# Memory keys of the last four sequences: transposed by VectorE inside one tile and scored on sixteen 32x32 tiles of the array, in place of TensorE transposes and column tiles; value products in two pieces

## The chip, the cores and the metric

The kernel runs on one core of a Trainium2 chip. The metric is device time in microseconds, the median of several runs. Engines are named as the profile names them: PE (TensorE matmul; PEld is its weight load), DVE (VectorE), ACT (ScalarE), POOL (GpSimd), SP (SyncE, which here mainly issues DMAs). Each has its own queue and takes its instructions strictly in the order of that queue.

## The reference, cut to what matters

The program is one layer of a decoder for a prompt group (1 sequence of 512 rows) and a sample group (8 sequences of 4 rows), with shared weights. The change touches the cross-attention alone, and there the sample group:

```python
def cross_attend(q, mk, mv):     # q (B, T, 4 heads, 256), mk and mv (B, 256 tokens, 4 heads, 256)
    s = einsum('bqhd,bmhd->bhqm', q, mk) * 256 ** -0.5
    return einsum('bhqm,bmhd->bqhd', softmax(s), mv)
```

For the prompt, `mk` and `mv` were computed earlier in the kernel. For each of the 8 sample sequences they lie in DRAM (`cache_mem_k`, `cache_mem_v`), 1 MB of keys and 1 MB of values each. A matmul contracts over the partitions, so the keys, which arrive with tokens on the partitions, must be turned so that the 256 dims of a head lie there.

## The kernel before, in words

The stage starts when the second half of the query projection ends and lasts until the output projection `w_mo`, whose first matmul in the trace is `mm<-wslot,oT`. Two streams of work are interleaved.

**The prompt** runs through a pipe of eight items (4 heads by 2 row blocks), one item a step at `next(prompt)`. `ch_soft` (L1357) makes 12 matmuls into `sca` (L1367), a row maximum on DVE (`cnm`, L1370), two exponentials on ACT (L1373), a reciprocal `csu` (L1374) and two multiplications `cp` on DVE (L1376). `ch_turn` (L1378) turns the result with 4 PE transposes `cpt` (L1385) and splits it into two parts with ACT and DVE (`pT`, L146 and L147). `ch_out` multiplies with the values (`cpo`, L1397) and evicts into `oT`.

**The samples**: `mk_load` (L1404) loads half a sequence's keys, 128 tokens x 1024, into a stage buffer `wst` (6 of them). `mk_turn` (L1409) turns that half with 8 PE transposes of 128x128 into `tpk` (L1416), copied into `kT` by ACT and DVE in turn (L1417). `kT` lives in the pool of weight slots, `W`, with four buffers. `mk_scores` (L1420) computes a sequence's scores with 8 matmuls on column tiles of the array, `128*32` in the profile (L1424). Then a maximum (`snm`, L1035) and an exponential (L1036). After the last sequence `sample_softmax` (L1039) turns and normalises the lot (`spa`, `spt`, `caz`). `mv_load` (L1428) loads values, for sequences 3 to 6 into slots of the same pool `W` (`vt`), else into stage buffers. `mv_out` (L1438) makes 8 matmuls a sequence into one accumulator `pso` (L1441). At the end ACT copies `pso` to `oS` (L1494) and PE turns it (`ost`, L1497) for the projection. 24 small loads (`cr`, L1509 to L1511) fetch convolution rows for the next sub-layer; they are issued by SP.

What sets the order: a tile scheduler places each instruction on its engine by a timeline of its own and by program order; `tc.issue_after` and `tc.high_priority` (the helper `burst`, L341) keep a group together behind a named instruction. PSUM banks come from two pools: `psm` with 5 banks (`sca`, `cpt`, `cpo`, `ssc`, `pso`) and `psa` with 3 (`tpk`, `spa`, `spt`, `ost`).

Of the kernel before, what the change touches and what calls it, by code (L numbers as in the profile page):

```python
# [18 lines left out]
NB = 8  # L19
# [58 lines left out]
def kernel(ctx: ExitStack, tc: tile.TileContext, I, O):  # L78
# [10 lines left out]

    cst = ctx.enter_context(tc.tile_pool(name="cst", bufs=1))  # L90
    sp = ctx.enter_context(tc.tile_pool(name="sp", bufs=11))
    wp = ctx.enter_context(tc.tile_pool(name="wp", bufs=NSLOT))
    stg = ctx.enter_context(tc.tile_pool(name="stg", bufs=6))
    npool = ctx.enter_context(tc.tile_pool(name="npool", bufs=5))
    t2p = ctx.enter_context(tc.tile_pool(name="t2p", bufs=8))
    zp = ctx.enter_context(tc.tile_pool(name="zp", bufs=3))
    sm = ctx.enter_context(tc.tile_pool(name="sm", bufs=4))
    psm = ctx.enter_context(tc.tile_pool(name="psm", bufs=5, space=bass.MemoryType.PSUM))
    psa = ctx.enter_context(tc.tile_pool(name="psa", bufs=3, space=bass.MemoryType.PSUM))
    dram = ctx.enter_context(tc.tile_pool(name="dram", bufs=1, space=bass.MemoryType.DRAM))  # L100
# [109 lines left out]
        return stg.tile([P, 1024], F32, name="wst", tag="st")  # L210

    def slot_tile():
        return wp.tile([P, 2, 1024], F32R, name="wslot", tag="W")

    def split_w(sv, st, share):

# [821 lines left out]
    def sample_softmax(sall, su, coef, sel, oname):  # L1038


        cf = small(NB, "scf")
        nc.vector.reciprocal(out=cf, in_=su)
        if coef is not None:
            VTS(out=cf, in0=cf, scalar1=coef, scalar2=None, op0=MUL)
        VTT(out=cf, in0=cf, in1=sel, op=MUL)
        VTT(out=view(csz, 0, [(64, NB // 2), (48, 2), (1, 16)]),
            in0=con("comb").unsqueeze(1).unsqueeze(1).broadcast_to([P, NB // 2, 2, 16]),
            in1=cf.rearrange("p (i e) -> p i e", e=2).unsqueeze(3).broadcast_to([P, NB // 2, 2, 16]), op=MUL)
        az = S([P, 2, H, NB * NS], F32, oname + "z")
        nc.gpsimd.memset(az, 0.0)  # L1050
        w = sall.shape[2]
        pa = at("spa")
        for e in range(2):
            for i in range(NB // 2):
                mm(pa[NS * i:NS * i + NS, :w], lhsT=csz[:, 2 * i + e, :], rhs=sall[:, 2 * i + e, :], start=(e == 0), stop=(e == 1))
        a = Z("spc")[:, :w]
        nc.scalar.copy(out=a, in_=pa[:, :w])
        pT = at("spt")
        for g in range(2):
            tr(pT[:, g * P:(g + 1) * P], a[:, g * P:(g + 1) * P], ident)  # L1060
        for g in range(2):
# [274 lines left out]
    qs = sm.tile([P, 8, NS], F32, name="qs", tag="qz", bufs=1)  # L1336
    qh, ql = [], []

    def ev_q(m):
        if m % 2 == 0:  # L1340
            qh.append(npool.tile([P, 2, 516], F32R, name="qh", tag="N"))
        if m % 4 == 0:
            ql.append(S([P, 4, SEQ], F32R, "ql"))

        def ev(i, c0, c1, ps):
            n = min(c1, SEQ) - c0
            q = qh[m // 2][:, m % 2, c0:c0 + n]
            nc.scalar.mul(out=q, in_=ps[:, :n], mul=1.0 / 16.0)
            STT(out=ql[m // 4][:, m % 4, c0:c0 + n], in0=ps[:, :n], scalar=1.0 / 16.0, in1=f32(q), op0=MUL, op1=SUB)
            if i == 1:  # L1350
                nc.scalar.mul(out=qs[:, m, :], in_=ps[:, n:n + NS], mul=1.0 / 16.0)
        return ev
# [3 lines left out]

    pTs, cps = {}, {}  # L1357

    def ch_soft(i):
        h, bp = i // 2, i % 2  # L1360
        sv = v2(mmp("sca"), 256)
        for j in range(2):
            t0 = (2 * bp + j) * P
            for c in range(2):
                q, l = qh[h][:, c, t0:t0 + P], ql[h // 2][:, 2 * (h % 2) + c, t0:t0 + P]
                for m, (x, k) in enumerate(((q, 0), (q, 1), (l, 0))):
                    mm(sv[:, j, :], lhsT=x, rhs=mkT[k][:, 2 * h + c, :], start=(c + m == 0), stop=(c == 1 and m == 2))  # L1367
        nm = small(2, "cnm")
        su = small(2, "csu")
        VRED(out=nm, in_=sv, axis=AX.X, op=MAX, negate=True)  # L1370
        p = cps[i] = v2(Z("cp"), 256)
        for j in range(2):
            ACT(out=p[:, j, :], in_=sv[:, j, :], func=AF.Exp, bias=nm[:, j:j + 1], accum_out=su[:, j:j + 1])  # L1373
        nc.vector.reciprocal(out=su, in_=su)  # L1374
        for j in range(2):
            VTS(out=p[:, j, :], in0=p[:, j, :], scalar1=su[:, j:j + 1], scalar2=None, op0=MUL)  # L1376
# [27 lines left out]
    def mk_load(i):  # L1404
        b, c = i // 2, i % 2
        kst[i] = stage()
        dma(out=kst[i], in_=I["cache_mem_k"][0, b, c * P:(c + 1) * P].rearrange("t h d -> t (h d)"))

    def mk_turn(i):  # L1409
        b, c = i // 2, i % 2  # L1410
        if c == 0:
            kts[b] = wp.tile([P, 8, 256], F32, name="kT", tag="W")
        for q in range(2):
            ps = at("tpk")
            for j in range(4):
                t = tr(ps[:, j * P:(j + 1) * P], kst[i][:, (4 * q + j) * P:(4 * q + j + 1) * P], ident)  # L1416
            (VCP if q else nc.scalar.copy)(out=kts[b][:, 4 * q:4 * q + 4, c * P:(c + 1) * P], in_=v2(ps, P))  # L1417
        return t.ins

    def mk_scores(b):  # L1420
        ps = mmp("ssc")[:, :256]
        for c in range(2):
            for h in range(H):
                t = mm(ps[NS * h:NS * h + NS], lhsT=qs[:, 2 * h + c], rhs=kts[b][:, 2 * h + c, :], start=(c == 0), stop=(c == 1))  # L1424
        sample_exp(sall, b, ps, nm, su)
        return t.ins

    def mv_load(b):  # L1428

        if 2 < b < 7:  # L1430
            t = wp.tile([P, 2, DM], F32, name="vt", tag="W")
            vts[b] = [t[:, 0], t[:, 1]]
        else:
            vts[b] = [stage(), stage()]
        for c in range(2):
            dma(out=vts[b][c], in_=I["cache_mem_v"][0, b, c * P:(c + 1) * P].rearrange("t h d -> t (h d)"))

    def mv_out(b):  # L1438
        for c in range(2):
            for h in range(H):  # L1440
                t = mm(pso[NS * h:NS * h + NS], lhsT=az[c][:, h, b * NS:(b + 1) * NS], rhs=vts[b][c][:, 256 * h:256 * h + 256],  # L1441
                       start=(b == 0 and c == 0), stop=(b == NB - 1 and c == 1))
# [51 lines left out]
    nc.scalar.copy(out=oS, in_=pso)  # L1494
# [10 lines left out]
    conv0 = I["state_conv"][0].rearrange("b j c -> (b j) c")

    def conv_in(t, p0, o, c0, n):

        dma(out=t[p0:p0 + 16, o:o + n], in_=conv0[:, c0:c0 + n])  # L1509
        dma(out=t[p0 + 16:p0 + 19, o:o + n], in_=I["w_dw"][0][:, c0:c0 + n])  # L1510
        dma(out=t[p0 + 19:p0 + 20, o:o + n], in_=I["b_dw"][:, c0:c0 + n])  # L1511


    cr = N("cr")
    for g in range(6):
        conv_in(cr, 20 * g, 0, 896 * g + (64 if g > 2 else 0), 896)
    conv_in(cr, 0, 896, 2688, 64)
    conv_in(cr, 0, 960, 5440, 64)
# [359 lines left out]
```

## Time and profile before

| quantity | value |
|---|---|
| time, median of 3 runs | 958.68 us (957.56 to 959.15) |
| time of the profiled execution | 957.37 us |
| its span in the trace | 955.6 us |
| from the first `sca` of this stage to the first `w_mo` matmul | 437.41 to 491.42 us |
| mean granted PE clock of the execution | 0.994 |

The span is what the profiler saw between the first and the last instruction; 1.8 us of the execution lie outside it. In a group line, the number behind `x` counts instructions, then come busy time and the mean duration of one in ns, then the idle time of the engine just before them with what ended it. In a timeline line, the first number is the start, the second the time until the last of the run of instructions ended. A matmul of fp32 is recorded as two passes, so 64 records are 32 matmuls. Records of matmuls overlap at their ends, so the cost of a run of them is read from its start to the next row's start.

### The profile page before, as it was taken

Reading aid. Unit: us, or ns where it says so; the run is one execution under the profiler, and the core shown is the slowest. Engines: PE = TensorE matmul, PEld = TensorE weight load, DVE = VectorE, ACT = ScalarE, POOL = GpSimd, SP = SyncE. Lnnn points to the kernel's source line nnn. Section 1 sums busy time; section 2 is a strip of 40 time slices with the busy share of each in tenths; the row PEclk is TensorE's granted clock in tenths of the full one; section 3 lists DMA queues with packets and bytes.
Section 4 is the critical chain, followed back from the end, with each engine's and each line's share of the span. In section 5 each row is a group of like instructions: output and inputs, shape, how many; then the busy total and the mean of one; then the engine's idle time right before and its main releaser. Section 6 shows DMA issues by size and latency. Waiting matters only on the chain. (4 is left out here: it accounts for less than half of the span.)

```text
span 955.6 us, 17087 instructions
## 1 busy us (share of the span) xinstructions
PE 933.3 (98%) x6619; PEld 810.2 (85%) x6619; DVE 600.3 (63%) x1129; ACT 387.7 (41%) x750; POOL 196.4 (21%) x383
## 2 busy tenths in 40 slices
PE   8999999999999999999999999999999999999995
PEld 5899787889766778998767799989988997999974
DVE  6745145565886448635654769727758676676767
ACT  5655134344676357635544523332212222222232
POOL 6610000115432216300000454001110110110114
PEclk9999999999999999999999999999999999999998
DMA  8950023344825539946954743063053313512023
GB/s 296 296 178 1 1 88 136 88 131 137 275 82 171 173 100 346 289 137 188 344 195 115 206 133 88 4 177 89 4 144 82 119 26 81 162 48 89 24 92 116
DMA packets 120674, 130.27 MB, mean 136 GB/s; under 512 B 8568, under 2 KB 86233, under 8 KB 120593
## 3 DMA queue, kind: packets, MB, share of 16 engines
q1 hardware_dynamic: 114408, 125.69, 42.3%
q10 hardware_dynamic: 6184, 3.48, 1.2%
q8 instruction: 52, 0.85, 0.4%
q14 instruction: 30, 0.24, 0.1%
HBM read 112.22 MB, written 16.93 MB: 135 GB/s over the span
## 5 line engine op out<-in xcount | busy, mean ns | idle before, releaser
L146 ACT CAST wslot<-wst 128x1024 fp32r<-128x1024 f32 x125 | 130.8, 1050 | 261.3 <-issue 73.5
L477 PE MATMUL mm<-fT,wslot 128*128 128x256 f32 x1872 | 235.9, 288 | 0.0
L477 PEld LDWEIGHTS mm<-fT,wslot 128*128 128x128 f32 x1872 | 234.4, 188 | 1.8 <-issue 0.8
L147 DVE TENSOR_TENSOR wslot<-wst,wslot 128x1024 fp32r<-128x1024 f32 x125 | 154.4, 1238 | 91.8 <-ACT wslot L146 91.4
L1689 PE MATMUL mm<-wslot,act 128*128 128x512 f32 (+1 forms) x180 | 70.2, 391 | 0.0
L1690 PE MATMUL mm<-wslot,act 128*128 128x512 f32 (+1 forms) x180 | 70.0, 392 | 0.0
L1688 PE MATMUL mm<-wslot,act 128*128 128x512 f32 (+1 forms) x180 | 69.3, 387 | 0.0
L1596 POOL COPY cvo<-u 128x2 f32<-128x2 f32 x43 | 11.0, 256 | 204.7 <-DVE u L1594 194.6
L407 PE MATMUL mm<-wslot,hT 128*128 128x512 f32 x128 | 51.6, 403 | 0.0
L477 PE MATMUL mm<-hT,wslot 128*128 128x256 f32 (+1 forms) x384 | 51.0, 289 | 0.0
L409 PE MATMUL mm<-wslot,hT 128*128 128x512 f32 x128 | 51.0, 400 | 0.0
L408 PE MATMUL mm<-wslot,hT 128*128 128x512 f32 x128 | 50.7, 396 | 0.0
L1591 DVE TENSOR_TENSOR u<-mm,rsb 128x256 f32<-128x256 f32 x43 | 18.2, 424 | 51.0 <-PE mm L477 50.0
L477 PEld LDWEIGHTS mm<-hT,wslot 128*128 128x128 f32 x384 | 49.2, 188 | 0.5 <-issue 0.2
L1688 PEld LDWEIGHTS mm<-wslot,act 128*128 128x128 f32 x180 | 34.3, 191 | 8.0 <-issue 0.4
L1690 PEld LDWEIGHTS mm<-wslot,act 128*128 128x128 f32 x180 | 33.8, 188 | 7.2 <-issue 0.4
L1689 PEld LDWEIGHTS mm<-wslot,act 128*128 128x128 f32 x180 | 33.8, 188 | 7.2
L1608 ACT ACTIVATE c<-c 128x560 f32<-128x560 f32 x21 | 14.1, 672 | 56.5 <-DVE c L1602 56.5
L1602 DVE SCALAR_TENSOR_TENSOR c<-u,cvT,c 128x560 f32<-128x560 f32 x43 | 34.3, 798 | 0.9
L1601 DVE SCALAR_TENSOR_TENSOR c<-u,cvT,c 128x560 f32<-128x560 f32 x43 | 34.1, 793 | 0.2
L1701 DVE TENSOR_TENSOR yp<-mm,yp 128x512 f32<-128x512 f32 (+1 forms) x41 | 27.2, 674 | 5.1 <-PE mm L1690 5.0
L409 PEld LDWEIGHTS mm<-wslot,hT 128*128 128x128 f32 x128 | 24.1, 188 | 5.1
(474 smaller groups left out, 1863.8 us busy)
## 6 DMA issues: line engine op xcount, KB each, us to landing
wst<-in_w_up_dram SPq DMA_DIRECT2D x42, 512.0 KB
wst<-in_w_in_dram SPq DMA_DIRECT2D x28, 512.0 KB
wst<-in_w_down_dram SPq DMA_DIRECT2D x20, 512.0 KB
wst<-in_cache_mem_k_dram SPq DMA_DIRECT2D x16, 512.0 KB
wst<-in_w_mk_dram SPq DMA_DIRECT2D x8, 512.0 KB
xb<-in_x_prompt_dram SPq DMA_DIRECT2D x8, 512.0 KB
wst<-in_cache_dk_dram SPq DMA_DIRECT2D x16, 256.0 KB
wst<-in_cache_dv_dram SPq DMA_DIRECT2D x16, 256.0 KB
```

Source lines behind the costliest of these rows:

```text
L146: nc.scalar.copy(out=hi, in_=src)
L147: (eng or nc.vector).tensor_tensor(out=lo, in0=src, in1=f32(hi), op=SUB)
L407: mm(ps[b], lhsT=xt.hi(k, c0, c0 + n), rhs=s[:, 0, kk, :], start=(k == 0), stop=False)
L408: mm(ps[b], lhsT=xt.hi(k, c0, c0 + n), rhs=s[:, 1, kk, :], start=False, stop=False)
L409: return mm(ps[b], lhsT=xt.lo(k, c0, c0 + n), rhs=s[:, 0, kk, :], start=False, stop=(k == nk - 1))
L477: mm(ps[i], lhsT=s[:, l, k, :], rhs=x(k, c0, c1), start=(k == 0 and j == 0), stop=(k == 7 and j == 2))
L1601: STT(out=c, in0=u[:, 1:EXT - 1], scalar=w[1], in1=c, op0=MUL, op1=ADD)
L1602: STT(out=c, in0=u[:, 0:EXT - 2], scalar=w[0], in1=c, op0=MUL, op1=ADD)
L1688: mm(ps, lhsT=t[:, 0, c0:c0 + P], rhs=s[:, 0, i % 2, cs], start=st, stop=False)
L1689: mm(ps, lhsT=t[:, 0, c0:c0 + P], rhs=s[:, 1, i % 2, cs], start=False, stop=False)
L1690: return mm(ps, lhsT=t[:, 1, c0:c0 + P], rhs=s[:, 0, i % 2, cs], start=False, stop=en)
L1701: VTT(out=y, in0=ps, in1=y, op=ADD)
```

## The change

Keys of sequences 0 to 3 go as before. Behind their scores the pool of weight slots is closed, and one tile `kq` (128 partitions x 8 half sequences x 1024) is opened in its place. Eight loads bring the keys of sequences 4 to 7 into it with tokens on the partitions; eight DVE instructions turn it in place in blocks of 32x32. The queries `qs` are stored to DRAM and read back four times into `qrep`, which has every block of 32 dims at every quarter of the partitions. 128 matmuls of 32 x 32 (`ssq`) then contract over 32 dims each, on sixteen tiles of the array: the row group is the tokens' quarter, the column group the head. Four accumulators in four banks of `psm` receive them, and four copies, one reduction over the four sequences and four exponentials follow. Only then is the pool of slots opened again, and the values of sequences 3 to 6 can be loaded into it. The value products are issued in two runs, sequences 2, 1, 0 and then 7, 6, 5, 4, 3. The 24 `cr` loads are issued by ACT's queue during the query projection.

```diff
-    wp = ctx.enter_context(tc.tile_pool(name="wp", bufs=NSLOT))
+    opened("w", NSLOT)
+    ctx.callback(lambda: closed("w"))
...
+    def conv_rows(g):
+        p0, o, c0, n = (20 * g, 0, 896 * g + (64 if g > 2 else 0), 896) if g < 6 else (0, 896 + 64 * (g - 6), 2688 + 2752 * (g - 6), 64)
+        for q0, m, src in ((0, 16, conv0), (16, 3, I["w_dw"][0]), (19, 1, I["b_dw"])):
+            nc.scalar.dma_start(out=cr[p0 + q0:p0 + q0 + m, o:o + n], in_=src[:, c0:c0 + n])
...
+    def kq_load(b):
+        for c in range(2):
+            dma(out=kq[:, b - 4, c], in_=I["cache_mem_k"][0, b, c * P:(c + 1) * P].rearrange("t h d -> t (h d)"))
+
+    def kq_turn(b):
+        for c in range(2):
+            nc.vector.transpose(kq[:, b - 4, c], kq[:, b - 4, c])
+
+    def kq_scores(t):
+        ps = [mmp("ssq") for _ in range(4)]
+        kt = kq.rearrange("p b c (j r) -> p (b c) j r", r=NS)
+        for j in range(8):
+            for i in range(4):
+                r = slice(NS * i, NS * i + NS)
+                for h in range(H):
+                    with burst(t):
+                        t = mm(ps[i][NS * h:NS * h + NS, :256], lhsT=qrep[r, 2 * h + j // 4, j % 4, :], rhs=kt[r, :, 8 * h + j, :],
+                               start=(j == 0), stop=(j == 7)).ins
+        for i in range(4):
+            (VCP if i % 2 else nc.scalar.copy)(out=sall[:, 4:8, :].rearrange("p b (c i r) -> p b c i r", c=2, i=4)[:, :, :, i, :],
+                                               in_=ps[i][:, :256].rearrange("p (b c r) -> p b c r", c=2, r=NS))
+        VRED(out=nm[:, 4:8], in_=sall[:, 4:8, :], axis=AX.X, op=MAX, negate=True)
+        for b in range(4, 8):
+            ACT(out=sall[:, b, :], in_=sall[:, b, :], func=AF.Exp, bias=nm[:, b:b + 1], accum_out=su[:, b:b + 1])
...
     next(prompt)
     for b in range(4):
-        t = mk_scores(b)
-    with tc.issue_after(t):
-        for j in range(8, 16):
-            t = mk_turn(j)
-            if j + 6 < 2 * NB:
-                mk_load(j + 6)
-            if j == 11:
-                next(prompt)
-    for b in range(3):
-        mv_load(b)
-    next(prompt)
-    with tc.issue_after(t):
-        for b in range(4, NB):
-            t = mk_scores(b)
+        with tc.issue_after(t):
+            mk_scores(b)
+    mv_load(0)
+    closed("w")
+    opened("k", 1)
+    kq = lay["k"][1].tile([P, 4, 2, DM], F32, name="kq", tag="K")
+    for b in range(4, NB):
+        kq_load(b)
+    dma(out=qs_d, in_=qs)
+    for i in range(4):
+        dma(out=qrep[NS * i:NS * i + NS], in_=qs_d.rearrange("(j q) m n -> q m j n", q=NS))
+    mv_load(1)
+    mv_load(2)
+    for b in range(4, NB):
+        kq_turn(b)
+    for _ in range(5):
+        next(prompt)
+    kq_scores(pe_last[0])
+    closed("k")
+    opened("w", NSLOT)
     for b in range(3, 7):
         mv_load(b)
     next(prompt)
-    _, az = sample_softmax(sall, su, None, con("selX"), "ca")
+    with tc.high_priority():
+        _, az = sample_softmax(sall, su, None, con("selX"), "ca")
...
-    for b in range(4):
-        mv_out(b)
-        if b == 0:
-            mv_load(7)
+    mv_out(VORD[:6])
+    mv_load(7)
     W.pump()
     next(prompt, None)
     next(prompt, None)
-    for b in range(4, NB):
-        mv_out(b)
+    mv_out(VORD[6:])
     run(prompt)
```

What the scheduler makes of it is seen in the order of the instructions; names are those of the program, output on the left, inputs on the right, and line numbers belong to each kernel's own source. On PE before, behind the scores of sequences 0 to 3, the transposes and scores of sequences 4 to 7 stand in this way:

```order
L1424 MATMUL ssc<-kT,qs 32x256 x27
L1416 MATMUL tpk<-cpk,wst 128x128 x12
...
L1367 MATMUL sca<-mkT,ql 128x256
L1416 MATMUL tpk<-cpk,wst 128x128 x40
L1424 MATMUL ssc<-kT,qs 32x256 x32
L1385 MATMUL cpt<-cpk,cp 128x128 x4
```

On PE after, at the same place, the prompt's items follow the scores at once, and the scores of sequences 4 to 7 come five `sca` groups later:

```order
L1438 MATMUL tpk<-cpk,wst 128x128 x4
L1476 MATMUL ssc<-kT,qs 32x256 x32
...
L1407 MATMUL cpt<-cpk,cp 128x128 x4
...
L1407 MATMUL cpt<-cpk,cp 128x128
...
L1389 MATMUL sca<-mkT,ql 128x256
L1463 MATMUL ssq<-kq,qrep 32x256 x128
L1419 MATMUL cpo<-pT,mvN 128x512 x12
```

So PE loses 64 transposes, and between the scores of the first four sequences (`ssc`) and those of the last four (`ssq`) it has prompt work alone: in all 60 `sca`, 16 `cpt` and 12 `cpo` matmuls.

On DVE after, from the maxima of the first four sequences on, the turns of `kq` stand among the prompt's small operations:

```order
L1392 TENSOR_REDUCE cnm<-sca 128x2
L157 TENSOR_TENSOR pT<-cpt,pT 128x256
L1453 STREAM_TRANSPOSE kq<-kq 128x1024
L1396 RECIPROCAL csu<-csu 128x2
L1392 TENSOR_REDUCE cnm<-sca 128x2
L157 TENSOR_TENSOR pT<-cpt,pT 128x256
L1398 TENSOR_SCALAR cp<-cp,csu 128x256 x2
L1453 STREAM_TRANSPOSE kq<-kq 128x1024 x2
...
L1453 STREAM_TRANSPOSE kq<-kq 128x1024
L1392 TENSOR_REDUCE cnm<-sca 128x2
L157 TENSOR_TENSOR pT<-cpt,pT 128x256
L157 TENSOR_TENSOR oT_5287<-cpo,oT_5286 128x512 x2
```

The first turn stands ahead of the `csu` and `cp` of the prompt's second item, and the second group of `cpt` on PE (the single row behind `...` above) reads that `cp`. Before, DVE had a copy of 512 columns (`kT<-tpk`) at such places.

On SP (the DMA issues) after, the order is this; before, the `cr` loads stood between the key loads, and `vt` followed the first six value loads directly:

```order
L1429 DMA wst<-in_cache_mem_k_dram 128x1024 x8
L1488 DMA wst<-in_cache_mem_v_dram 128x1024 x5
L1526 DMA qs_d<-qs 128x256
L1488 DMA wst<-in_cache_mem_v_dram 128x1024
L1528 DMA qrep<-qs_d 32x32x32 x4
L1449 DMA kq<-in_cache_mem_k_dram 128x1024 x8
L1129 DMA xb<-x_d_2549 32x1024
L1129 DMA xb<-x_d_2549 128x1024 x2
L1488 DMA vt<-in_cache_mem_v_dram 128x1024 x8
L1129 DMA xb<-x_d_2549 128x1024
L1488 DMA wst<-in_cache_mem_v_dram 128x1024 x2
```

The loads of `kq` now stand behind the store and the four reads of the queries, and `vt` behind `kq`.

More of the change, by code (lines that the diff above doesn't have):

```diff
@@ L97, with opened, closed @@
     sm = ctx.enter_context(tc.tile_pool(name="sm", bufs=4))
+    lay = {}
+    def opened(key, bufs):
+        c = tc.tile_pool(name=f"{key}{len(lay)}", bufs=bufs, side="right")
+        lay[key] = (c, c.__enter__())
+    def closed(key):
+        lay[key][0].__exit__(None, None, None)
+    opened("w", NSLOT)
+    ctx.callback(lambda: closed("w"))
     psm = ctx.enter_context(tc.tile_pool(name="psm", bufs=5, space=bass.MemoryType.PSUM))
@@ L212, in slot_tile @@
     def slot_tile():
-        return wp.tile([P, 2, 1024], F32R, name="wslot", tag="W")
+        return lay["w"][1].tile([P, 2, 1024], F32R, name="wslot", tag="W")
     def split_w(sv, st, share):
@@ L1185, in dk_turn @@
     def dk_turn(b):
-        kt = kts[b] = wp.tile([P, H, 260], F32, name="kT", tag="W")
+        kt = kts[b] = lay["w"][1].tile([P, H, 260], F32, name="kT", tag="W")
         nc.gpsimd.tensor_copy(out=kt[:, :, 256:260], in_=dkT[:, :, SEQ + TS * b:SEQ + TS * (b + 1)])
@@ L1337 @@
     qh, ql = [], []
+    conv0 = I["state_conv"][0].rearrange("b j c -> (b j) c")
+    cr = N("cr")
+    def conv_rows(g):
+        p0, o, c0, n = (20 * g, 0, 896 * g + (64 if g > 2 else 0), 896) if g < 6 else (0, 896 + 64 * (g - 6), 2688 + 2752 * (g - 6), 64)
+        for q0, m, src in ((0, 16, conv0), (16, 3, I["w_dw"][0]), (19, 1, I["b_dw"])):
+            nc.scalar.dma_start(out=cr[p0 + q0:p0 + q0 + m, o:o + n], in_=src[:, c0:c0 + n])
     def ev_q(m):
@@ L1357 @@
     pTs, cps = {}, {}
+    pe_last = [None]
     def ch_soft(i):
@@ L1366, in ch_soft @@
                 for m, (x, k) in enumerate(((q, 0), (q, 1), (l, 0))):
-                    mm(sv[:, j, :], lhsT=x, rhs=mkT[k][:, 2 * h + c, :], start=(c + m == 0), stop=(c == 1 and m == 2))
+                    pe_last[0] = mm(sv[:, j, :], lhsT=x, rhs=mkT[k][:, 2 * h + c, :], start=(c + m == 0), stop=(c == 1 and m == 2)).ins
         nm = small(2, "cnm")
@@ L1411, in mk_turn @@
         if c == 0:
-            kts[b] = wp.tile([P, 8, 256], F32, name="kT", tag="W")
+            kts[b] = lay["w"][1].tile([P, 8, 256], F32, name="kT", tag="W")
         for q in range(2):
@@ L1418, in mk_turn @@
         return t.ins
+    qrep = S([P, 8, 4, NS], F32, "qrep")
+    qs_d = dram.tile([P, 8, NS], F32, name="qs_d")
+    def kq_load(b):
[20 more added lines that the diff above has]
+            ACT(out=sall[:, b, :], in_=sall[:, b, :], func=AF.Exp, bias=nm[:, b:b + 1], accum_out=su[:, b:b + 1])
     def mk_scores(b):
@@ L1430, in mv_load @@
         if 2 < b < 7:
-            t = wp.tile([P, 2, DM], F32, name="vt", tag="W")
+            t = lay["w"][1].tile([P, 2, DM], F32, name="vt", tag="W")
             vts[b] = [t[:, 0], t[:, 1]]
@@ L1436, in mv_load, with mv_out @@
             dma(out=vts[b][c], in_=I["cache_mem_v"][0, b, c * P:(c + 1) * P].rearrange("t h d -> t (h d)"))
-    def mv_out(b):
-        for c in range(2):
+    VORD = [(b, 1 - c if b in (2, 7) else c) for b in (2, 1, 0, 7, 6, 5, 4, 3) for c in range(2)]
+    def mv_out(bs):
+        t = None
+        for b, c in bs:
             for h in range(H):
-                t = mm(pso[NS * h:NS * h + NS], lhsT=az[c][:, h, b * NS:(b + 1) * NS], rhs=vts[b][c][:, 256 * h:256 * h + 256],
-                       start=(b == 0 and c == 0), stop=(b == NB - 1 and c == 1))
-        return t.ins
+                with burst(t):
+                    t = mm(pso[NS * h:NS * h + NS], lhsT=az[c][:, h, b * NS:(b + 1) * NS],
+                           rhs=vts[b][c][:, 256 * h:256 * h + 256], start=((b, c) == VORD[0]), stop=((b, c) == VORD[-1])).ins
     sall = S([P, NB, 256], F32, "cas")
@@ L1453 @@
             for j in (i // 2 - 1, i // 2):
-                mk_turn(j)
-                mk_load(j + 6)
+                t = mk_turn(j)
+                if j < 2:
+                    mk_load(j + 6)
+            conv_rows(i // 2 - 1)
+            conv_rows(i // 2)
     next(prompt)
     for b in range(4):
-        t = mk_scores(b)
-    with tc.issue_after(t):
-        for j in range(8, 16):
-            t = mk_turn(j)
-            if j + 6 < 2 * NB:
-                mk_load(j + 6)
-            if j == 11:
-                next(prompt)
-    for b in range(3):
-        mv_load(b)
-    next(prompt)
-    with tc.issue_after(t):
-        for b in range(4, NB):
-            t = mk_scores(b)
+        with tc.issue_after(t):
[18 more added lines that the diff above has]
+    opened("w", NSLOT)
     for b in range(3, 7):
@@ L1504 @@
     cvT = S([P, NUT, 20], F32, "cvT")
[L1505 to L1518, printed above, removed]
     for t0 in (0, 4):
```

## The prediction, on record before the changed kernel was run

> **What bounds the kernel now.** I read the busy shares first, then PE's waits, then the timeline of this stage on PE, DVE and SP.
>
> ```profile
> PE 933.3 (98%) x6619; PEld 810.2 (85%) x6619; DVE 600.3 (63%) x1129; ACT 387.7 (41%) x750; POOL 196.4 (21%) x383
> PE ost L1497 <- ACT oS L1494: 1.5, 1, 1.5
> 458.30:472.50 14.20, 14.20 (x107) 12.12 (x103) 10.11 (x26) 8.97 (x35) 0.00 (x0) 1.00 1.02 409
> ```
>
> PE is busy 98% of the span. In the middle of this stage (third line, a window of 14.20 us: PE, PEld, DVE, ACT, POOL busy, granted clock, DMA share, GB/s) it is busy all the time, and DVE for 10.1 us. So a microsecond taken off PE here is a microsecond of time, as long as nothing else becomes late. The only wait of note in the stage is 1.5 us at its end, for the eviction of the samples' output (second line). The DMA engines are full in that window, at 409 GB/s: 512 KB take 1.28 us there.
>
> **What PE loses.**
>
> ```profile
> 439.00 1.05 PE L1424 MATMUL ssc<-kT,qs 128*32 128x256 f32 x10
> 439.99 0.65 PE L1416 MATMUL tpk<-cpk,wst 128*128 128x128 f32 x4
> 440.57 3.22 PE L1424 MATMUL ssc<-kT,qs 128*32 128x256 f32 x54
> 443.72 1.53 PE L1416 MATMUL tpk<-cpk,wst 128*128 128x128 f32 x12
> 445.01 0.48 PE L1367 MATMUL sca<-mkT,qh 128*128 128x256 f32 x2
> 446.50 0.60 PE L1385 MATMUL cpt<-cpk,cp 128*128 128x128 f32 x4
> 446.86 0.48 PE L1367 MATMUL sca<-mkT,qh 128*128 128x256 f32 x2
> 447.18 0.60 PE L1416 MATMUL tpk<-cpk,wst 128*128 128x128 f32 x4
> 447.53 0.37 PE L1367 MATMUL sca<-mkT,ql 128*128 128x256 f32 x1
> 447.74 1.03 PE L1416 MATMUL tpk<-cpk,wst 128*128 128x128 f32 x8
> 448.53 0.48 PE L1367 MATMUL sca<-mkT,qh 128*128 128x256 f32 x2
> 449.68 5.09 PE L1416 MATMUL tpk<-cpk,wst 128*128 128x128 f32 x40
> 454.70 3.66 PE L1424 MATMUL ssc<-kT,qs 128*32 128x256 f32 x64
> 458.29 0.66 PE L1385 MATMUL cpt<-cpk,cp 128*128 128x128 f32 x4
> ```
>
> From start to the next start, the 64 transposes (rows of 12, 4, 8 and 40) take 1.29 + 0.35 + 0.79 + 5.02 = **7.45 us**, all removed. The 64 records of the last four sequences' scores take 3.59 us; `ssq` takes their place. The first four sequences' scores stand in two pieces of 0.99 and 3.15 us, 4.14 in all; in one piece they should take 3.59 too, a gain of **0.55**.
>
> ```profile
> 472.55 0.62 PE L1441 MATMUL pso<-wst,caz 128*32 128x256 f32 x2
> 473.10 0.55 PE L1385 MATMUL cpt<-cpk,cp 128*128 128x128 f32 x3
> 473.57 2.58 PE L1441 MATMUL pso<-wst,caz 128*32 128x256 f32 x43
> 477.16 0.66 PE L1385 MATMUL cpt<-cpk,cp 128*128 128x128 f32 x4
> 485.93 0.85 PE L1441 MATMUL pso<-vt,caz 128*32 128x256 f32 x11
> ```
>
> A piece of value products with 2 records takes 0.55 us, one with 62 (three rows more, up to 477.16) 3.59: 0.051 a record, and 0.45 for going to column tiles and back. There are six pieces, the last at 485.93; two remain, which saves 4 x 0.45 = **1.8**. The wait of 1.5 for `oS` goes too: `ost` stands behind 18 matmuls of `w_mo`. Together 7.45 + 0.55 + 1.8 + 1.5 = **11.3 us** off PE.
>
> `ssq` has 128 matmuls in 8 rounds of 16 tiles. A round of four column tiles (eight records) took 3.59 / 8 = 0.45 us; if all sixteen run beside each other, eight rounds take 3.59, no loss; if row groups run one after another, 4 x 3.59 = 14.4, a loss of 10.8. Between lies the issue of instructions:
>
> ```profile
> L962 PE MATMUL mlsi<-wst,qzm x64: 272/273/276, 230.1 to 231.7; 128*32 128x128 f32 x64
> ```
>
> 64 records in 1.6 us are 25 ns each, the fastest pace of small matmuls here; 256 records by it are 6.4 us, a loss of 2.8. I take no loss, since no row shows a limit there, and keep 2.8 and 10.8 for the range. The Trainium skill ("TensorE: Matmul & The Clock Gate", Part 3: Packing small matmuls) gives 10.6 times for 4x4 tiles and 3.07 times for four row tiles, so sixteen tiles would be 3.45 times as fast as four and `ssq` would take 4.2, an estimate 0.6 above mine; no run here shows sixteen tiles.
>
> **What replaces it.** The keys of the last four sequences can be loaded only when `ssc` has read the slots. In the new order 4 transposes (0.58) and then 64 records (3.59) follow 439.00: `ssc` ends at 443.2.
>
> ```profile
> 437.46 0.20 ACT L1351 ACTIVATE qs<-mm 128x32 f32<-128x32 f32 x1
> 474.26 1.80 SPq L1436 DMA_DIRECT2D wst<-in_cache_mem_v_dram  x2
> 474.20:475.20 1.00, 1.00 (x26) 0.61 (x20) 0.48 (x2) 1.00 (x5) 0.00 (x0) 1.00 0.06 16
> 475.20:476.20 1.00, 1.00 (x26) 0.57 (x22) 0.95 (x3) 0.04 (x1) 0.00 (x0) 1.00 0.96 147
> 476.20:477.20 1.00, 1.00 (x19) 0.41 (x11) 0.00 (x0) 0.00 (x0) 0.00 (x0) 1.00 0.86 352
> q10 hardware_dynamic: 2690, 1.98, 30.6%
> ```
>
> Two loads issued at 474.26 find the queues nearly empty; 16 + 147 + 352 KB have moved by 477.2, so a 512 KB load lands **2.9 us** after its issue. Ahead of `kq` stand the four reads of `qrep`, 4096 pieces of 128 B, 256 for each DMA engine. The last row (a queue in the DMA view of 40 to 60 us: packets, MB, share of 16 engines) prices a packet of 736 B: 0.306 x 16 x 20 / 2690 = 36 ns. One of 4 KB takes 160 at 409 GB/s. The line through both gives 14 ns at 128 B, 3.6 us in all; ends are 1.3 (by bytes) and 9.3 (36 ns each). `qs` is complete at 437.7; its store lands about 2.5 later, the reads flow some 2.3 after their issue, so they end at 442.5 + 3.6 = 446.1, and the first half of `kq` lands 1.3 later, **447.4**. By the ends: 446.1 and 453.1.
>
> DVE's first turn stands ahead of the `csu` and `cp` of the second item, and DVE works in order, so everything behind it waits for that landing.
>
> ```profile
> L147 DVE TENSOR_TENSOR wslot<-wst,wslot 128x1024 fp32r<-128x1024 f32 x125 | 154.4, 1238 | 91.8 <-ACT wslot L146 91.4
> L318 DVE TENSOR_SCALAR hN<-xb,rs 128x1024 f32<-128x1024 f32 x4 | 3.0, 751 | 2.3 <-POOL rs L304 2.3
> L1370 DVE TENSOR_REDUCE cnm<-sca 128x2 f32<-128x512 f32 x8 | 5.5, 690 | 3.7 <-PE sca L1367 3.6
> L147 DVE TENSOR_TENSOR pT<-cpt,pT 128x256 fp32r<-128x256 f32 x15 | 6.2, 421 | 4.1 <-ACT pT L146 3.9
> L1376 DVE TENSOR_SCALAR cp<-cp,csu 128x256 f32<-128x256 f32 x16 | 5.1, 350 | 0.2
> L1374 DVE RECIPROCAL csu<-csu 128x2 f32<-128x2 f32 x8 | 1.3, 161 | 1.2 <-ACT cp L1373 0.9
> 442.47 0.61 DVE L1376 TENSOR_SCALAR cp<-cp,csu 128x256 f32<-128x256 f32 x2
> ```
>
> No row shows a turn. I take the row of the same shape, 1.24 us, since the turn reads and writes 1024 elements of 4 bytes; the lower end is 0.75, the one-source row; the upper, by the 690 ns for 512 elements, is 1.38. Two `cp` of 0.35 take 0.61 together, so 0.09 of each instruction lies in the next one. A turn then costs 1.15, eight 9.2. Between the first and the last stand 3 `csu`, 2 `cnm`, 3 `pT`, 6 `cp`: 0.48 + 1.38 + 1.26 + 2.10 - 14 x 0.09 = 4.0. DVE runs without a gap from 447.4 to 447.4 + 13.2 = **460.6**. Then `ssq` needs four of the five banks of `psm`, which come free with one `cnm`, three `pT`, two `oT` (by the 690 row) and a `csu`: 2.9 more, **463.5**.
>
> PE has work for less. From 443.2 on: 60 `sca` (12 take 446.50 - 445.01 = 1.49, so 7.45), 16 `cpt` (4 take 0.36, so 1.44), 12 `cpo` (2.94 from this row):
>
> ```profile
> 468.14 2.94 PE L1397 MATMUL cpo<-pT,mvN 128*128 128x512 f32 x12
> ```
>
> Together 11.8: it would reach `ssq` at 455.0. It **idles 8.5 us** before `ssq`; the first part, from 443.2 + 1.49 + 0.36 + 1.49 = 446.5 to the first `cp` at 449.8, is one gap of 3.3.
>
> Behind `ssq` the chain to `spa` (two copies a side, a maximum over 1024 columns, four exponentials, `csz`) is about 4.8 us long, beside 4.7 of `cpo`, `cpt` and `sca`. The last two value loads (sequence 7) wait for stage buffers of the first run of products, land 3.8 later (2.9 + half of 1.80), and their products stand 1.7 behind that run: a wait of 0.4 to 2.1, by when the buffers come free. With the casts of `w_mo` behind them I take **1.5**, from 0.5 to 3. The `vt` loads start after `ssq`, at 467, take 8 x 1.28 + 2.9 and land by 481, some 2 us before their products: hidden; later landing of `kq` moves both. The `cr` loads cost ACT 24 issues of about 0.3 in the query projection, where ACT stood idle 5.73 us before a pair of evictions:
>
> ```profile
> 436.25 0.66 ACT L1348 ACTIVATE qh<-mm 128x256 fp32r<-128x256 f32 x2 [5.73 <-PE mm L477]
> ```
>
> Nothing for that. **Sum:** -11.3 + 8.5 + 1.5 = -1.3. The profiled execution took 957.37 (span 955.6, and 1.8 around it), so 956.1 by it; the median stands 1.3 higher at 958.68, so 957.4 by that. I predict **957.5**. The PE work removed is nearly all given back as waiting for DVE.
>
> **Rivals.** *Faster, about 954*: turns at 0.75 take 8 x 0.49 = 3.9 off DVE's chain, and the idle before `ssq` falls to 4.6. For it: a one-source row has that pace. Against it: a turn is no plain stream, and `cnm` with one source runs at 1.35 ns an element. Same sign, smaller: `qrep` done early, -1.3.
>
> *Slower, up to 963*: the small pieces of `qrep` hold up `kq`. Each us that the first half lands behind 447.4 is a us of PE's idle; from 450.5 on the kernel is slower by over 0.2%, and 453.1 gives +5.7. For it: 128 B is far below any packet that I could price; against: the reads are issued some 2 us before `kq`.
>
> *The change doesn't do what it says*: the sixteen tiles don't run together, +2.8 to +10.8, 960.3 to 968.3. The rows show four column tiles together, but no row groups.
>
> *The clock falls.*
>
> ```profile
> 6.00:8.20 2.20, 0.49 (x5) 0.25 (x3) 1.77 (x4) 1.73 (x5) 1.03 (x3) 1.00 1.08 342
> 8.20:11.60 3.40, 2.93 (x11) 2.69 (x12) 2.17 (x4) 2.67 (x6) 3.26 (x3) 0.51 1.04 386
> ```
>
> After a stretch in which PE did little, its granted clock stood at 0.51 for 3.4 us. After the gap of 3.3 the same would add at most half of 3.4, 1.7, but PE waits for DVE there anyway, so I expect 0 to 0.5 of it: 957.5 to 959.2. The Trainium skill (the same page, "Why this matters for your kernels") asks for no idle gaps of PE above about 3 us, and so speaks against this change; the rows above agree with it.
>
> **How the numbers follow.** Forecast 0.42 (955 to 960), faster rival 0.24, `qrep` 0.19, tiles 0.10, clock 0.05. About 0.2%, 1.9 us, is what a measurement can tell. Faster by more is below 956.8: 0.13 of the forecast and 0.22 of its rival, 0.35. Slower is above 960.6: 0.02, 0.17, 0.10 and 0.01, 0.30. The rest, 0.35, is the same. The range goes from 951.5 (cheap turns and no wait behind `ssq`) to 966 (slow `qrep` and the issue pace of `ssq` together).
>
> **What would show it.** Steps hold if `tpk` shrinks by 64 matmuls, PE waits once for 3 to 4 us for `cp` behind the first turn, DVE is gapless over eight turns of 1.1 to 1.3 us, `ssq` starts near 463 and takes 3.6 to 4.2 us, `pso` has two pieces, and `ost` no wait. It is wrong if the first turn starts after 449, if `ssq` takes over 5, if a turn is far from 1.24, or if PE waits over 3 us behind `ssq`.

## The result, and the profile after

| kernel | median us (lowest to highest) | against before | 95% interval |
|---|---|---|---|
| before | 958.89 (957.56 to 961.23) | | |
| changed | 965.98 (964.67 to 967.18) | 1.0072 | 1.0054 to 1.0089 |

The change makes the kernel slower by 7.1 us (0.7%). 957.5 was forecast; 965.98 lies at the upper edge of the range (966.0), on the other side of no change. The profiled execution of the changed kernel took 964.67 us, with a span of 962.9. One execution of a later experiment, e3, took 3218.84 us and is left out of its median.

The traces of the two kernels give a second measure. At the first `w_mo` matmul the kernel before still has ten `cpo` matmuls open and the changed kernel none, so the stage is better read from the start of the first `sca` to the end of the last `w_mo` matmul:

```profile
545.05 0.40 PE L409 MATMUL mm<-wslot,oT 128*128 128x512 f32 x1
551.99 0.39 PE L419 MATMUL mm<-wslot,oT 128*128 128x512 f32 x1
```

That is 545.45 - 437.41 = 108.04 us before (first line) and 552.38 - 439.40 = 112.98 after: 4.9 us of the 7.3 between the two profiled executions. The rest lies ahead of the stage (2.0) and behind it (0.4).

Three of PE's waits in the stage of the changed kernel (line waited at, what it waited for, us in total, times, longest). None of them was there before, and the 1.5 us for `ost` are gone:

```profile
PE cpt L1407 <- DVE cp L1398: 5.6, 1, 5.6
...
PE pso L1498 <- DMA wst<-in_cache_mem_v_dram: 1.2, 1, 1.2
...
PE ssq L1463 <- issue: 0.7, 1, 0.7
```

The timeline of PE in the stage shows where they lie:

```profile
439.40 0.48 PE L1389 MATMUL sca<-mkT,qh 128*128 128x256 f32 x2
...
441.44 3.66 PE L1476 MATMUL ssc<-kT,qs 128*32 128x256 f32 x64
445.03 0.51 PE L1389 MATMUL sca<-mkT,qh 128*128 128x256 f32 x2
...
448.31 0.28 PE L1389 MATMUL sca<-mkT,ql 128*128 128x256 f32 x1
454.15 0.45 PE L1407 MATMUL cpt<-cpk,cp 128*128 128x128 f32 x1 [5.56 <-DVE cp L1398]
454.25 0.78 PE L1389 MATMUL sca<-mkT,qh 128*128 128x256 f32 x2
...
468.49 4.64 PE L1463 MATMUL ssq<-kq,qrep 32*32 32x256 f32 x213
473.82 1.31 PE L1463 MATMUL ssq<-kq,qrep 32*32 32x256 f32 x43 [0.69 <-issue]
475.06 3.04 PE L1419 MATMUL cpo<-pT,mvN 128*128 128x512 f32 x12
...
493.70 1.07 PE L1498 MATMUL pso<-wst,caz 128*32 128x256 f32 x16 [1.15 <-DMA wst<-in_cache_mem_v_dram]
```

The 64 transposes are gone and the first scores stand in one piece (445.03 - 441.44 = 3.59). Then PE stands still for 5.6 us, until `cp` of the second item is there. `ssq` runs from 468.49 to 475.06, 6.57 us where 3.59 were forecast, with a break of 0.69 in it. `pso` waits 1.15 for sequence 7.

The starts of the single `ssq` records in the trace show where the 6.57 us go. Of the 255 steps from one start to the next, 240 are at most 60 ns long, 13.4 on average, close to the 14.0 that the forecast implies (3.59 / 256). The other 15, of 67 to 1059 ns, take 3.0 us together. So the sixteen tiles do work beside each other, but the stream stops. The longest, 1.06 us between the starts of the 213th record and the next, is the row with `issue`: PE waited for nothing that the profile shows. A DMA queue shows what it probably was:

```profile
q8 instruction: 53, 0.87, 0.4%
```

The count of this queue (packets, MB, share of 16 engines) goes with PE's instructions: 52 packets of 16 KB in the kernel before, where PE and PEld have 13238 instructions, and 53 here, where they have 256 more. One packet moved from 471.38 to 472.32, while `ssq` ran, and the stream resumes 1.5 us after it, at 473.82. The other six profiles with a whole `ssq` show the same: the stream resumes 1.3 to 1.5 us after a packet of this queue has landed. In e4, where 24 more matmuls stand ahead, the stop comes 25 records earlier. So PE most likely waited for its own next instructions. What makes the 14 shorter stops is open.

Why `cp` is late is read from SP and DVE. SP's issues (start, us until the last of the group is issued):

```profile
439.67 0.37 SPq L1526 DMA_DIRECT2D qs_d<-qs  x1
441.54 0.33 SPq L1488 DMA_DIRECT2D wst<-in_cache_mem_v_dram  x1
443.52 3.25 SPq L1528 DMA_DIRECT2D qrep<-qs_d  x4
446.94 4.13 SPq L1449 DMA_DIRECT2D kq<-in_cache_mem_k_dram  x8
```

and DVE's timeline, with the first and the last of the eight turns:

```profile
451.53 1.25 DVE L1453 STREAM_TRANSPOSE kq<-kq 128x1024 f32<-128x1024 f32 x1 [3.42 <-DMA kq<-in_cache_mem_k_dram]
452.70 0.12 DVE L1396 RECIPROCAL csu<-csu 128x2 f32<-128x2 f32 x1
452.75 0.67 DVE L1392 TENSOR_REDUCE cnm<-sca 128x2 f32<-128x512 f32 x1
453.33 0.41 DVE L157 TENSOR_TENSOR pT<-cpt,pT 128x256 fp32r<-128x256 f32 x1
453.66 0.60 DVE L1398 TENSOR_SCALAR cp<-cp,csu 128x256 f32<-128x256 f32 x2
...
457.20 0.69 DVE L1392 TENSOR_REDUCE cnm<-sca 128x2 f32<-128x512 f32 x1 [0.60 <-PE sca L1389]
...
464.08 1.24 DVE L1453 STREAM_TRANSPOSE kq<-kq 128x1024 f32<-128x1024 f32 x1
```

The four reads of the queries take SP 3.25 us to issue, 0.81 each, where `kq`'s eight take 4.13. Ahead of them SP stood still for 1.6 us, until the store `qs_d` had landed. So the first key load is issued at 446.94, 1.9 us after `ssc` ended, and lands 4.6 later, at 451.5. From there DVE works without a gap, but for 0.60, until 465.3; three operations of the prompt stand behind the first turn ahead of the `cp` that PE waits for. A turn takes 1.24 us, as forecast.

The windows of the gap and of what follows it (length, then PE, PEld, DVE, ACT and POOL busy, granted clock, DMA share, GB/s):

```profile
448.60:454.15 5.55, 0.00 (x0) 0.03 (x1) 2.62 (x6) 0.89 (x4) 0.00 (x0) 0.90 1.02 357
454.15:463.20 9.05, 8.59 (x32) 7.06 (x33) 8.45 (x14) 1.99 (x8) 0.00 (x0) 0.50 0.89 319
```

Behind the gap PE's granted clock is halved for 9 us (two `sca` take 0.78 instead of 0.48). DVE is busy for 8.45 of these 9.05 us, so little of it should reach the end; e4 tests that.

### The profile page after: what moved, and what is told of

Read it like the earlier page. It is cut to its first block, busy times and chain, and to the rows that moved or that the text cites. A ratio compares the mean times of both kernels' runs of the same rounds, so it can differ in the third digit from the quotient of the medians.

```text
span 962.9 us, 17322 instructions
## 1 busy us (share of the span) xinstructions
PE 932.9 (97%) x6747; PEld 808.6 (84%) x6747; DVE 602.9 (63%) x1128; ACT 384.2 (40%) x744; POOL 198.0 (21%) x383
## 4 chain that ended last, share of the span: by engine, by line
PE 80%; DVE 7%; DMA 6%; ACT 3%; issue 2%; POOL 1%; SPq 1%; DVEq 0%; ACTq 0%; POOLq 0%
PE mm L487 32%; PE mm L475 7%; PE mm L417 6%; PE mm L418 6%; PE mm L419 6%; PE mm L1739 3%; PE mm L1737 3%; PE mm L1738 3%; DMA wst<-in_w_mk_dram 2%; PE mm L396 1%; DVE wslot L157 1%; PE sda L1221 1%; DMA kq<-in_cache_mem_k_dram 1%; PE sdn L396 1%; PE oda L1247 1%
## 5 line engine op out<-in xcount | busy, mean ns | idle before, releaser
L314 POOL TENSOR_TENSOR rs<-ssy,mhalf 128x1 f32<-128x1 f32 (+1 forms) x10 | 6.4, 639 | 107.6 <-DVE ssy L1139 104.7
```

## The experiments

Times are medians, against the kernel before in the same series (958.9 to 959.3). "To ssq" is the time from the first `sca` of the stage to the first `ssq` in that kernel's profile, "ssq" from there to the next matmul, "stage" the time from the first `sca` to the end of the last `w_mo` matmul. The stage is one execution's; the two kernels that differ in the convolution loads alone, before and e8, agree in it to 0.04 us, while the times of single executions of one kernel spread over 2 to 8.

| kernel | us | against before, 95% interval | to ssq | ssq | stage |
|---|---|---|---|---|---|
| before | 958.89 | | | | 108.04 |
| changed | 965.98 | 1.0072 (1.0054 to 1.0089) | 29.1 | 6.6 | 112.98 |
| e2, keys issued first | 962.75 | 1.0033 (1.0021 to 1.0046) | 26.5 | 6.9 | 112.73 |
| e3, turns late | 963.57 | 1.0044 (1.0027 to 1.0061) | 27.3 | 7.8 | 112.55 |
| e4, gap filled | 964.41 | 1.0055 (1.0038 to 1.0072) | 28.7 | 6.8 | 112.10 |
| e5, ssq on half the columns | 970.40 | 1.0102 (1.0075 to 1.0128) | 29.5 | 7.1 | 119.23 |
| e9, half of the ssq matmuls | 961.67 | 1.0028 (1.0012 to 1.0043) | 29.4 | 3.3 | 109.37 |
| e11, keys and loads alone | 964.70 | 1.0062 (1.0039 to 1.0084) | 28.9 | 7.2 | 112.90 |
| e7, three mends | 960.56 | 1.0016 (1.0001 to 1.0031) | 25.7 | 6.4 | 108.61 |
| e1, value products alone | 957.91 | 0.9986 (0.9976 to 0.9995) | | | 105.72 |
| e6, e1 with sequence 7 last | 959.20 | 0.9998 (0.9984 to 1.0012) | | | 106.01 |
| e10, e1 with sequence 7 third | 957.62 | 0.9985 (0.9971 to 1.0000) | | | 105.39 |
| e8, convolution loads alone | 958.57 | 0.9993 (0.9976 to 1.0009) | | | 108.08 |

**The late landing: e2.**

```diff
     for i in range(4):
-        dma(out=qrep[NS * i:NS * i + NS], in_=qs_d.rearrange("(j q) m n -> q m j n", q=NS))
+        with tc.issue_after(kq_last[0]):
+            dma(out=qrep[NS * i:NS * i + NS], in_=qs_d.rearrange("(j q) m n -> q m j n", q=NS))
```

> The changed kernel with the four reads of the queries issued behind the eight key loads instead of ahead of them. Theory (late first landing): the first key load is issued when the scores of sequences 0 to 3 end (445.0 on the scale of the changed kernel's trace) and lands 2.9 us later, near 448 instead of 451.5; DVE is gapless from there, so the time falls by about 3.5 us to 962.5, and PE's wait for cp shrinks from 5.6 to about 2. Rival (DVE or the DMA rate bounds the turns whenever the first one lands, or the queries then come too late): 965 to 967.

SP and DVE in this kernel's timeline:

```profile
444.16 3.79 SPq L1449 DMA_DIRECT2D kq<-in_cache_mem_k_dram  x8
448.06 11.59 SPq L1531 DMA_DIRECT2D qrep<-qs_d  x4
```

```profile
447.85 1.25 DVE L1455 STREAM_TRANSPOSE kq<-kq 128x1024 f32<-128x1024 f32 x1 [0.86 <-DMA kq<-in_cache_mem_k_dram]
```

The first load is issued 0.2 us after `ssc` ends (at 443.9 there) and lands 3.7 later, where it was 1.9 and 4.6. PE's wait for `cp` falls to 3.0, and `ssq` starts 2.6 earlier. So the theory holds on the landing: the reads issued ahead of the keys made it late. What it gave at the end is less clear. The median falls by 3.2 us, close to the 3.5 expected, but in the trace the stage is only 0.25 shorter, because PE then waits 3.2 us for the values of sequence 7 instead of 1.15:

```profile
PE pso L1500 <- DMA wst<-in_cache_mem_v_dram: 3.2, 1, 3.2
```

Why the medians differ by more than this is not settled.

**The place of the turns: e3.**

```diff
-    for b in range(4, NB):
-        kq_turn(b)
     for _ in range(5):
         next(prompt)
+    for b in range(4, NB):
+        with tc.issue_after(cp_last[1]):
+            kq_turn(b)
```

> The changed kernel with the eight turns on DVE allowed only behind the cp of the prompt's second item. Theory (the length of DVE's chain from the first landing to the last turn decides): only some 1.2 to 1.6 us of small operations move ahead of the landing, so 964 to 965, though PE's single wait of 5.6 us breaks up. Rival (the blocked queue itself is the loss): the 5.6 us come back, near 960.5.

The single wait is gone, but new ones stand in its place on PE:

```profile
PE cpo L1421 <- DVE pT L157: 2.9, 1, 2.9
PE sca L1389 <- DVE kq L1455: 2.6, 1, 2.6
...
PE cpt L1409 <- DVE cp L1398: 1.5, 2, 1.1
```

2.4 us of the median come back, not 5.6, and `ssq` starts 1.8 earlier: the length of DVE's chain counts, and only what can be moved ahead of the landing shortens it. `ssq` itself, which starts at half clock and stops twice, takes 1.2 of the 1.8 back, and in the trace the stage is only 0.4 shorter.

**The halved clock: e4.** After the third `sca` group PE got 24 matmuls that nothing reads.

```diff
+        if k == 1:
+            gps = at("gap")
+            g = pe_last[0]
+            for _ in range(24):
+                with burst(g):
+                    g = mm(gps, lhsT=warm[:, 0:P], rhs=warm, start=True, stop=True).ins
```

> The changed kernel with 24 matmuls of 128x512 bf16 on zeros, without use, put on PE into the wait for the second item's cp, so that PE does not stand idle there. Theory (PE waits for DVE in this stretch whatever its clock): the granted clock stays at 1.0 behind the gap instead of 0.50 for 9 us, and the time falls by 1 us at most, 965 to 966. Rival (the halved clock is what the change loses): the 4.5 us of PE work lost at half clock come back, 961 to 962.

The row of e4 behind the gap (length, PE busy, granted clock, DMA share, GB/s):

```profile
458.00:462.00 4.00, 3.09 (x12) 0.72 0.78 221
```

The granted clock was 1.00 from 446 to 458 and 0.72 in the next 4 us, behind a wait of 1.6. The time fell by 1.6 us, which is more than the theory's 1 and far from the rival's 4.5; its interval overlaps with that of the changed kernel, and the scheduler moved a few prompt matmuls too. In the trace `ssq` starts 0.4 us earlier and the stage is 0.9 shorter, of which 0.8 is a shorter wait for sequence 7 (0.33). So by this run the clock costs at most 1.6 us, and by its trace less than 1.

**What ssq costs: e5 and e9.**

```diff
-                        t = mm(ps[i][NS * h:NS * h + NS, :256], lhsT=qrep[r, 2 * h + j // 4, j % 4, :], rhs=kt[r, :, 8 * h + j, :],
+                        t = mm(ps[i][NS * h:NS * h + NS, :128], lhsT=qrep[r, 2 * h + j // 4, j % 4, :], rhs=kt[r, 0:4, 8 * h + j, :],
```

> The changed kernel with each of the 128 ssq matmuls on 128 columns instead of 256: it leaves out the scores of sequences 6 and 7 and uses those of 4 and 5 in their place, so that only the time of ssq changes. Theory (the pace of issue bounds ssq: 256 records at about 22 to 25 ns each, whatever their columns): ssq stays near 6 us, from 5.5, and the time at 965 to 966. Rival (the columns are streamed, row groups partly one after another): ssq falls to about 3.3, and the time by some 3 us to 963.

PE in e5:

```profile
469.82 3.80 PE L1463 MATMUL ssq<-kq,qrep 32*32 32x128 f32 x213
475.65 1.35 PE L1463 MATMUL ssq<-kq,qrep 32*32 32x128 f32 x43 [2.03 <-issue]
```

213 records take 3.80 us, 17.8 ns each, against 4.64 and 21.8 on 256 columns. These two can't be compared as they stand, for the granted clock (the third number from the end) was not the same; the first line is from e5, the second from the changed kernel:

```profile
469.80:475.70 5.90, 3.87 (x222) 3.40 (x225) 1.48 (x4) 1.02 (x4) 0.00 (x0) 0.79 0.27 92
468.49:475.06 6.57, 5.88 (x257) 3.81 (x256) 2.31 (x7) 1.48 (x6) 0.00 (x0) 1.00 0.27 85
```

In e5 it stood at 0.50 for the first 2.2 us of `ssq`. The records 113 to 208 ran at full clock in both kernels; by their starts they follow each other at 13.1 ns in e5 and at 20.2 in the changed kernel. Half the columns save a third there, so the columns count too, and neither the theory nor the rival is right about the pace. All of `ssq` takes 7.1 us even so: the stop behind the 213th record grew from 1.06 to 2.30 us, and the first part ran at half clock. The packet of instructions starts to move 3.1 us into `ssq`, as late as in the changed kernel (2.9), but PE is then at its 184th record instead of its 145th, so that it runs out sooner. The time rose by 4.4 us, which neither foresaw. The granted clock behind `ssq` is 0.50, where it is 1.00 in the changed kernel:

```profile
477.00:481.00 4.00, 4.00 (x10) 3.14 (x11) 1.72 (x3) 2.35 (x10) 0.00 (x0) 0.50 0.69 206
```

That the longer stop lost the clock here is likely, since PE stood still for 2.03 us just ahead of it, but no run separates it from the rest.

```diff
-        for j in range(8):
+        for j in range(4):
...
-                               start=(j == 0), stop=(j == 7)).ins
+                               start=(j == 0), stop=(j == 3)).ins
```

> The changed kernel with half of the ssq matmuls, 64 of 256 columns: it leaves out the second half of the dims in the scores of sequences 4 to 7. Theory (ssq is on the path, and each of its records costs 21.8 ns, 5.6 us for 256, with a break of 0.7 us in its stream of instructions): 2.8 to 3.5 us less, 962.5 to 963.2. Rival (what waits behind ssq takes it up, or a slower granted clock does, as with half the columns): 965 or more.

```profile
467.58 3.35 PE L1463 MATMUL ssq<-kq,qrep 32*32 32x256 f32 x128
470.86 3.04 PE L1419 MATMUL cpo<-pT,mvN 128*128 128x512 f32 x12
```

128 records take 3.28 us, 3.3 us less than the whole, though the granted clock was 0.50 for almost half of that time (1.45 us). The time falls by 4.3 and the stage by 3.6: `ssq` is on the path in full. e9 has no wait for sequence 7, which was 1.15.

**The value products: e1, e11, e6 and e10.** e1 is the kernel before with `mv_out` in two runs and `mv_load(7)` between them, as in the change; e11 is the changed kernel with the loops of before.

> The kernel before with the value products alone as in the change (two runs of 24 and 40 matmuls, last load of sequence 7 behind the first run); keys as before. Theory (a piece costs 0.45 us): four pieces fewer give -1.8 us, and the wait for sequence 7's values, 1.15 us in the changed kernel, takes most of it back: 957.5 to 959 beside 958.9. Rival (pieces are free, only the wait counts): 960 or more.

> The changed kernel with the value products of the kernel before, so that the keys and the convolution loads alone are changed. Theory (the value products gave 1.4 us to the kernel before, and as much here): 966 + 1.4 = 967.4. Rival (the wait of 1.15 us for sequence 7 takes the gain back, here where all loads are late): 965 to 966.

In e1 two rows of PE show the runs, `ost` has no wait, and the second run waits for sequence 7:

```profile
471.97 2.80 PE L1446 MATMUL pso<-wst,caz 128*32 128x256 f32 x48
...
478.26 1.07 PE L1446 MATMUL pso<-wst,caz 128*32 128x256 f32 x16 [0.91 <-DMA wst<-in_cache_mem_v_dram]
479.15 3.63 PE L1446 MATMUL pso<-vt,caz 128*32 128x256 f32 x64
...
486.30 0.44 PE L1498 MATMUL ost<-cpk,oS 128*128 128x128 f32 x2
```

It gains 1.4 us on the kernel before, and its stage is 2.3 shorter. In the changed kernel the same edit gains nothing that can be measured: without it the time is 964.7, not 967.4, just below the rival's 965 to 966, and the stage is 112.90, not 112.98. e6 and e10 change the order of the second run:

```diff
-    VORD = [(b, 1 - c if b in (2, 7) else c) for b in (2, 1, 0, 7, 6, 5, 4, 3) for c in range(2)]
+    VORD = [(b, 1 - c if b == 2 else c) for b in (2, 1, 0, 6, 5, 4, 3, 7) for c in range(2)]
```

> The kernel before with the two runs of value products of e1, and sequence 7 last in the second run instead of first. Theory (the second run waits 0.9 us for sequence 7's values because it begins with them): the wait goes, and the time falls by 0.9 below e1, to about 957. Rival (a projection weight cast or the values of another sequence is late next): no change against e1, 957.9.

The wait for sequence 7 goes, and a wait of 1.37 for `pT` takes its place, behind four casts of `w_mo` on ACT. Nothing of e1's gain is left in the median, though the stage is only 0.3 longer than in e1:

```profile
488.95 0.84 PE L1397 MATMUL cpo<-pT,mvN 128*128 128x512 f32 x2 [1.37 <-ACT pT L146]
```

With sequence 7 third (`2, 1, 0, 6, 5, 7, 4, 3`):

> The kernel before with the two runs of value products of e1, and sequence 7 third in the second run. Theory (e1 waits 0.9 us for sequence 7, e6 waits 1.4 us for pT behind four casts of w_mo; with sequence 7 in the middle neither is whole): 957 to 958. Rival (PE runs into one of the two anyway): 958 to 959.5.

957.62: a wait of 0.87 for `pT` remains, and e10 can't be told from e1. e1 is 0.14% faster than the kernel before and e10 0.15%, with an interval that reaches 1.0000; no other version is faster than both kernels, and both keep the keys of before.

**The convolution loads: e8**, the kernel before with `conv_rows` on ACT's queue.

> The kernel before with the 24 small convolution loads alone moved from SP to ACT's queue, as in the change. Theory (they are hidden on either queue): no difference, 958 to 960. Rival (ACT's issues delay the evictions of the query projection, which is why the changed kernel's stage began 2 us later): 961.

No difference in the time or in the stage (108.08 us, 108.04 before). The query projection itself, from its first matmul to the first `sca`, takes 55.6 us in both.

**All mends: e7** joins e2, e3 and the order of e6.

> The changed kernel with the key loads ahead of the reads of the queries (e2), the turns behind the second item's cp (e3) and sequence 7 last in the second run. Theory (first landing 3.5, DVE's chain 1.2, and a wait of 1.2 to 3.2 for sequence 7's values, each by itself on the path): 966 - 3.5 - 1.2 - 2 = about 959.5, equal to the kernel before within 1.5 us, since ssq's 6.6 us and DVE's chain remain. Rival (the mends overlap and DVE's chain of turns bounds all of it): 962 or more.

960.56, 5.4 us below the changed kernel and 1.4 above before; the theory said 959.5. In the trace its stage takes 108.6 us, 4.4 less than in the changed kernel and 0.6 more than before. The mends need each other there: e2 and e3 by themselves shorten the stage by 0.25 and 0.4, as their gain is lost again in the wait for sequence 7 or in `ssq`; in e7, with sequence 7 last, that wait is 0.4.

## Why the prediction was wrong, point by point

- **What PE loses: right in size.** Transposes, the joined `ssc` piece, two runs of `pso` and no wait for `ost` are all as described. But the 1.8 us of the runs did not arrive in this kernel (e11), as the wait for sequence 7 stands between them. The term of 1.5 for the waits behind `ssq` measured 1.15 for sequence 7, 0.46 for `pT` and 0.33 for `spc`, 1.9 together.
- **"`ssq` takes their place ... I take no loss, since no row shows a limit there": this step failed.** `ssq` cost 6.57 instead of 3.59, and e9 shows that it is on the path. That the sixteen tiles run beside each other was right (one after another by row groups would be 14.4 us), and between its stops the stream has the pace of the forecast. What the sum had at nothing were the stops, 3.0 us together, the longest of 1.06 most likely a wait for PE's own instructions. The 25 ns a record of `mlsi`, which would have made 6.4, came close by luck: in that row the records start 7 ns apart in fours, with 89 ns between the fours, so it shows no pace of issue. The estimate of 4.2, made by figures of the Trainium skill ("TensorE: Matmul & The Clock Gate", Part 3: Packing small matmuls), is too low here by 2.4 us.
- **The landing of the first half of `kq`: mis-sized, by the wrong queue.** The prediction priced the reads of `qrep` on the DMA engines alone and took nothing for SP, which spends 3.25 us on their four issues. They also began later than reckoned: 3.85 us after the issue of the store, where 2.5 were taken. So SP reaches `kq` 1.9 us after the slots are free, and counted from the stage's first `sca` the landing came at 12.1 us instead of 10.0. In e2 the key loads are issued 1.7 us earlier and land 0.9 faster, so the reads cost something on the DMA engines too. The slower rival named the right mechanism, `qrep` holding up `kq`, but put most of its price in the wrong place.
- **DVE's chain: right.** A turn is 1.24 us, the chain from first to last turn 13.8 us (forecast 13.2; the 0.6 is a wait for `sca` at half clock), the banks 3.2 (2.9). `ssq` started at 29.1 us from the first `sca`, forecast 26.1: 2.1 for the landing, 0.6, 0.3.
- **The clock: happened, longer than thought.** 0.50 for 9 us, not 3.4. The cover was named rightly: DVE was busy meanwhile. 0.6 us are visible, and e4 bounds the whole at 1.6.
- **The sum.** Against the forecast for the profiled execution (956.1) it took 964.67, 8.6 more. In the stage that is 112.98 - (108.04 - 1.3) = 6.2: 3.0 before `ssq`, 3.0 in it, 0.3 behind it. Another 2.0 lie ahead of the stage and 0.4 behind it. The 2.0 are there already at the first matmul of the query projection (383.77 instead of 381.78), ahead of every instruction that the change adds, so none of the steps above makes them. Where they come from, and why the medians nevertheless miss by the same 8.5, is not settled.

Two of the signs named for a wrong forecast came true: the first turn started after 449 (451.5, or 449.5 with the stage's later start taken off), and `ssq` took over 5. The sign of the change followed from the size: a gain of 11.3 set against losses estimated at 10.0 leaves 1.3, and the two new things on the path, `ssq` and the way to the first landing, were priced 3.0 and 2.1 below what they cost.

## What to carry to other kernels

Work taken off a saturated engine counts only if the engine that takes it over has its inputs in time: follow the first piece of data through every queue that it passes, and price a DMA by what its issue costs the queue as well as by its bytes. Spreading the same work over more tiles adds instructions: the tiles may overlap as hoped, and the stream still stops, as `ssq` did at the edge of its loaded instructions. Before a pace is compared between two kernels, compare the granted clock, and read a mend from the stage in the trace as well as from the time: a wait further on can take it back (e2). A forecast that is the small difference of two large sums should take its sign from the pessimistic row of each new operation.

## What the runs showed of the hardware that was not expected

- An issue of a DMA in 1024 pieces of 128 B took SP 0.81 us, of 128 pieces of 4 KB 0.52 (3.25 / 4 and 4.13 / 8). Behind the eight key loads (e2) the same four reads took 11.59 us to issue.
- 32x32 matmuls of fp32 on 256 columns went out at 20.2 ns a record at full clock and at 31.6 at half clock (records 113 to 208 in the changed kernel, 1 to 96 in e11), on 128 columns at 13.1 and 18.4 (the same records, both in e5).
- In all seven profiles with 256 records of `ssq`, PE stopped at the same place of its instructions, behind the 212th or 213th record and in e4 behind the 188th, and went on 1.3 to 1.5 us after 16 KB of instructions had landed. From one start to the next the stop lasted 0.35 us in e4, which had stood still before, 0.40 in e11, whose first 3.3 us ran at half clock, 0.89 to 1.29 in four others and 2.30 on half the columns (e5).
- The length of a gap on PE did not set how long the granted clock stayed halved. Behind a gap of 3.0 us (e2) it was 0.50 for 9.0 us just as behind one of 5.6, though PE was busy for 8.54 of them; behind one of 5.0 (e9) it was 0.50 for 3.4:

```profile
450.50:459.50 9.00, 8.54 (x31) 7.01 (x32) 8.39 (x14) 1.96 (x8) 0.00 (x0) 0.50 0.96 288
451.96:455.37 3.41, 2.99 (x14) 3.02 (x15) 2.86 (x6) 0.74 (x4) 0.00 (x0) 0.50 1.02 411
```
